# A decoder layer on one core: a ring of ten weight parts, a seventh seven-product chunk, and one norm tile moved off VectorE

## The chip, the cores and the metric

The kernel runs on one core of a Trainium2 chip. The metric is the device time of one execution in microseconds (us). Engines are called PE (TensorE, the matrix engine), DVE (VectorE), ACT (ScalarE), POOL (GpSimd) and SP (SyncE, which here only issues DMAs). "L159" is line 159 of the kernel before.

## The reference

One layer for 256 tokens of width 1024, with 256 memory tokens and an inner width of 2816. Each of its three parts ends in a residual sum and a layer norm:

```python
z = h @ w_in                                  # pooling inputs u, and q, k, v of the attention
mix = concat(multiscale_pool(u), moba_attention(q, k, v)) @ w_out
h = layer_norm(ALPHA * h + mix, ln1_g, ln1_b)
h = layer_norm(ALPHA * h + memory_cross_attention(h, mem, w_xq, w_xkv, w_xo), ln2_g, ln2_b)
h = layer_norm(ALPHA * h + (silu(h @ w_gate) * (h @ w_up)) @ w_down, ln3_g, ln3_b)

def layer_norm(x, g, b):
    mu = mean(x, -1); var = mean((x - mu) ** 2, -1)
    return (x - mu) * rsqrt(var + 1e-5) * g + b
```

All arrays are float32.

## The kernel before, in words

**Products.** A float32 product is made of three PE products in a format that keeps fewer bits: each operand is cast to a high part (`h` in the names), the rest is its low part (`l`), and high x high, high x low and low x high are added in PSUM (`three`, L328 to L330). So every weight must be split before PE can use it: ACT casts the high part (L157) and DVE subtracts it from the original (L159).

**The stream of weights.** The class `Stream` (object `ws`) treats all weights as one list of numbered parts of 512 KB, 128 partitions x 1024. Part i is fetched by a DMA that SP issues into a raw tile `w{i}r` (a ring of seven), and split into `w{i}h` and `w{i}l` (a ring of `W_BUFS` = 8). `ws.prepare(n)` issues the splits up to part n, and the kernel calls it with `ws.used + AHEAD`, where `used` counts the parts with which PE is done, and `AHEAD` is 8. So the split of part i waits for PE's last product with part i-8. Small loads, as those of norm vectors, are hung in front of a part's fetch (`ws.before`).

**Gate and up.** Parts 59 to 102 hold the gate and up weights of the chunks c = 0 to 10 (256 of the 2816 inner columns each; four parts to a chunk). `proj_both` runs a chunk in phases: a group of rows first with the high parts (L775), then with the low parts (L781). A part counts as used in the low phase only. The group is all eight rows for most chunks and two rows for the last two. While PE works on a chunk, DVE and ACT finish the one before: `Gated.add` (L929, L930), `multiply` (L934, L935), and `split` (L391, L392), which gives the two parts of the activations of the chunk. Tokens go in two tiles of 128, t = 0 and 1.

**Down.** The down weights of a chunk are two parts, and a chunk costs 24 products of 128x512 (`eight`). For a chunk in the tuple `SEVEN`, the 2x2 block product (two token tiles by two halves of the columns) is instead done in seven block products of sums of blocks, so 21 PE products (`seven`). Its weights then need sums, which `prepare_pair` makes: three ring parts and a corner tile `w{i}c`, with eight DVE operations (L125 to L136) in place of two. `Gated.split` makes the sums of its activations (L946 to L949) and splits them too. Chunks are taken in the order `DOWN`. The last three, `LAST`, are plain and are kept for the end.

**The tail.** When the other chunks are done, DVE forms the residual plus the shared block products (L1061 to L1074). Meanwhile PE runs `pieces`: the six last parts for tile 0's lower and upper half, for tile 1's lower half, and for two quarters of tile 1's upper half. The first of these pieces is the first to use a last part, so it needs all six splits. As each piece ends, DVE adds it (L1090) and takes its statistics (L675). When a tile is complete, `finish` runs `stats` (L680, L682 on DVE, then the power -1/2 on POOL, L683, which gives `rs`), `centre` (L688: subtract the mean, multiply by g), `scale` (L693, in three pieces: multiply by `rs`, add b) and the stores (L986).

**Order.** The program is written out in order for each engine, and each engine takes its instructions strictly in that order; waits follow from the tiles' data and from the rings. Activations live in a ring of eleven tiles of 8 KB a partition (`a8`), smaller ones in rings of their own. The norm's vectors g and b and its two rows `r` have a pool of their own (`nmp`), in the space that the `early` pool gives back before the mix.

Of the kernel before, what the change touches and what calls it, by code (L numbers as in the profile page):

```python
# [24 lines left out]
NFC = DFF // CW  # L25
# [15 lines left out]


# [4 lines left out]
class Stream:  # L47
# [3 lines left out]
    def __init__(self, nc, pool):  # L51
        self.nc, self.pool = nc, pool
        self.pairs, self.corner = {}, {}
        self.src, self.raws, self.tiles, self.homes = [], [], [], []
        self.loads, self.splits = {}, {}
        self.used, self.held = 0, True
        self.pace, self.asked = 1, 0
        self.cuts, self.casts = {}, {}

    def add(self, src, parts=2):  # L60

# [23 lines left out]
    def fetch(self, upto, queue):  # L85

        while len(self.raws) < min(upto, len(self.src)):
            i = len(self.raws)
            for load in self.loads.pop(i, []):
                load()  # L90
            src = self.src[i]
            if src is None:
                self.raws.append(None)
                continue
            if i < len(self.homes):
                raw = self.homes[i]
            else:
                raw = self.pool.tile(list(src.shape), F32, tag="raw", name=f"w{i}r", bufs=RAW_BUFS)
            for s, q in self.cuts.get(i, [(slice(None), queue)]):
                q.dma_start(raw[:, :, s], src[:, :, s])  # L100
            self.raws.append(raw)

    def fetch_ahead(self):

# [33 lines left out]
    def prepare(self, upto, eng=None):  # L138
        nc = self.nc
        while len(self.tiles) < min(upto, len(self.src)):  # L140
            i = len(self.tiles)
            src = self.src[i]
            for split in self.splits.pop(i, []):
                split()
            self.fetch(i + 1, nc.sync)
            raw = self.raws[i]
            shape = list((self.src[i - 1] if src is None else src).shape)
            hi = self.pool.tile(shape, F32R, tag="hi", name=f"w{i}h")
            lo = self.pool.tile(shape, F32R, tag="lo", name=f"w{i}l")
            if i in self.pairs:  # L150
                self.prepare_pair(i, hi, lo)
                self.tiles.append((hi, lo))
                self.fetch_ahead()
                continue
            for group in self.casts.get(i, [[slice(None)]]):
                for s in group:
                    nc.scalar.copy(hi[:, :, s], raw[:, :, s])  # L157
                s = slice(group[0].start, group[-1].stop)
                (eng or nc.vector).tensor_sub(lo[:, :, s], raw[:, :, s], r32(hi[:, :, s]))  # L159
            self.tiles.append((hi, lo))  # L160
            self.fetch_ahead()

    def next(self):

        if not self.held:
            self.prepare(min(self.used + AHEAD, len(self.tiles) + 1))

    def get(self, numbers, k):

        n = self.src[numbers[0]].shape[1]  # L170
        self.prepare(numbers[k // n] + 1)
        self.asked += 1
        if not self.held and self.asked % self.pace == 0:
            self.prepare(min(self.used + AHEAD, len(self.tiles) + 1))
        return self.parts_of(numbers, k)

    def parts_of(self, numbers, k):
# [16 lines left out]
def decoder_layer(  # L194
# [24 lines left out]
    ws = Stream(nc, wp)  # L219
# [29 lines left out]
    c_gu = [ws.add(w_gu[c], 4) for c in range(NFC)]  # L249
    c_dn = {}  # L250
# [37 lines left out]
        nc.sync.dma_start(wpl, w_pool)  # L288
        nc.sync.dma_start(psc, pool_scale)

    gb = {}
# [360 lines left out]


    early.close()
    nmp = ctx.enter_context(tc.tile_pool(name="norm", bufs=1))


    class Norm:
        def __init__(self, i, tok, dst=None):
# [31 lines left out]
        def scale(self, c0, c1):  # L691
            s = slice(c0, c1)
            nc.vector.scalar_tensor_tensor(self.dst[:, s], self.r[:, s], self.rs, gb["b", self.i][:, s],  # L693
                                           op0=OP.mult, op1=OP.add)
# [11 lines left out]
    def project(chunks, get, held, pieces=PIECES):  # L706

        acc = {piece: accbank("acc") for piece in PIECES}  # L710
        if pieces != PIECES:
            (*_, (_, _, c), _), last = pieces, PIECES[-1]
            acc[pieces[-2]], acc[pieces[-1]] = acc[last][:, :c - last[1]], bank("acc")[:, :last[2] - c]
        head, rest = chunks[:-held], chunks[-held:]
        done = sum(ws.rows(numbers) for numbers in head)
        if head:
            yield from proj_rows(acc, head, get, PIECES, True, pieces != PIECES, True)
        ws.prepare(ws.used + AHEAD)
        ws.prepare(ws.used + W_BUFS, nc.gpsimd)
# [15 lines left out]
    h1 = ap.tile([P, T, D], F32, tag="a8", name="h1")  # L735
    mix = project(c_mix, lambda k: (cT[0][:, k], cT[1][:, k]), 4)
    for t in range(T):
        norm = Norm(1, xt[:, t, :], h1[:, t, :])
        for half in HALVES:
            norm.add(*half, until(mix)[1])  # L740
        norm.finish()
# [105 lines left out]
    h2T = Both("h2T")  # L847
# [11 lines left out]
    xattend(3)  # L859


    norm = Norm(2, h1[:, 0, :], h2[:, 0, :])
    for half in HALVES:
        norm.add(*half, until(xo)[1])
    norm.finish()
    norm = Norm(2, h1[:, 1, :], h2[:, 1, :])
# [17 lines left out]
    def gated_parts(c):  # L884


        if c in SEVEN:
            t = ap.tile([P, 2, 8, P], F32R, tag="a8", name=f"g{c}")
            gT[c] = t[:, 0], t[:, 1]
            return  # L890
        i, j = divmod([c for c in sorted(DOWN) if c not in SEVEN].index(c), 2)
        if j == 0:
            shared[i] = ap.tile([P, 2, 8, P], F32R, tag="a8", name=f"go{i}")
        gT[c] = tuple(shared[i][:, n, 4 * j:4 * j + 4] for n in range(2))

    def gated_pair(c, k, t):

# [87 lines left out]
    def store(t, y, c0, c1, queue=nc.sync):  # L985
        queue.dma_start(out[t * P:(t + 1) * P, c0:c1], y[:, c0:c1])  # L986
# [68 lines left out]


    lower, upper = slice(0, 512), slice(512, D)
    norms = [Norm(3, h2[:, t, :]) for t in range(T)]

    def with_residual(t, s, y):  # L1060
        nc.vector.scalar_tensor_tensor(norms[t].r[:, s], h2[:, t, s], ALPHA, y, op0=OP.mult, op1=OP.add)  # L1061
# [16 lines left out]
    def finish(norm, t):  # L1078

        norm.stats()  # L1080
        norm.centre(0, D)
        norm.scale(0, 512)
        store(t, norm.r, 0, 512)
        norm.scale(512, 768)
        store(t, norm.r, 512, 768, nc.scalar)
        norm.scale(768, D)
        store(t, norm.r, 768, D)

    def add(norm, c0, c1, acc):
        nc.vector.tensor_add(norm.r[:, c0:c1], acc, norm.r[:, c0:c1])  # L1090
# [69 lines left out]
```

## Time and profile before

| | |
|---|---|
| time, median of 3 runs | 379.52 us (379.52 to 379.84) |
| profiled execution | 380.66 us, its span 378.9 us, so 1.76 us lie around the span |
| granted PE clock, mean | 0.992 |
| PE busy | 368.3 us, 97% of the span, 2154 instructions |
| DVE busy | 303.1 us, 80%, 475 instructions |
| ACT busy | 200.3 us, 53%, 316 instructions |
| POOL busy | 20.4 us, 5%, 31 instructions |
| DMA | 71.95 MB, mean 190 GB/s |

A row of the timeline gives the start of an instruction within the span, its length, engine, line, operation, output and inputs, and in brackets how long its engine had been idle before it and what it waited for. Lengths of neighbours overlap a little, so the cost of one among many is the distance of two starts. In the rows of groups, the numbers behind the bar are the busy time of all and the mean length of one in ns.

### The profile page before, as it was taken

What the parts mean: (1) busy time and instruction counts of PE and PEld (TensorE: products, weight loads), DVE (VectorE), ACT (ScalarE), POOL (GpSimd) and SP (SyncE); (2) the same over time, 40 slices, a digit from 0 to 9 for tenths busy, and PEclk for the clock granted to TensorE, in tenths of its full rate; (3) what the DMA queues carried; (4) which work ended last, traced back from release to release, by engine and by line L of the source; (5) the groups of instructions that cost most, each with busy time, mean ns of one, the idle gap of its engine ahead of it and who ended that gap; (6) DMA issues with size and microseconds to landing.
All of it is one profiled execution on the core that took longest, in us unless ns stands there. A gap on an engine that the chain in (4) does not pass through costs nothing.

```text
span 378.9 us, 5741 instructions
## 1 busy us (share of the span) xinstructions
PE 368.3 (97%) x2154; PEld 323.3 (85%) x2154; DVE 303.1 (80%) x475; ACT 200.3 (53%) x316; POOL 20.4 (5%) x31
## 2 busy tenths in 40 slices
PE   8999999999999999999999999999999999999990
PEld 7997989998888889998878888888888888888880
DVE  4867889955599677865889787778886998999995
ACT  4746678643254645644147666555665565456400
POOL 1000035300020000000100000000000000000011
PEclk9999999999999999999999999999999999999996
DMA  8997683759508963343107855566554663364002
GB/s 263 412 411 252 205 293 129 228 179 299 191 3 270 390 215 123 113 161 112 61 3 240 331 171 173 196 222 220 193 167 163 260 221 111 111 222 136 32 35 78
DMA packets 21324, 71.95 MB, mean 190 GB/s; under 512 B 2480, under 2 KB 3504, under 8 KB 21168
## 3 DMA queue, kind: packets, MB, share of 16 engines
q1 hardware_dynamic: 20720, 71.05, 54.5%
q10 hardware_dynamic: 576, 0.52, 0.4%
q8 instruction: 17, 0.28, 0.3%
q14 instruction: 11, 0.09, 0.1%
HBM read 70.52 MB, written 1.05 MB: 189 GB/s over the span
## 4 chain that ended last, share of the span: by engine, by line
PE 90%; DVE 5%; ACT 1%; DMA 1%; POOLq 0%; POOL 0%; SPq 0%; issue 0%; DVEq 0%; ACTq 0%
PE pg L775 19%; PE pg L781 10%; PE pxk L346 6%; PE pqk L462 5%; PE pxq L775 4%; PE acc L328 4%; PE acc L329 4%; PE acc L330 4%; PE pu L346 3%; PE m L330 3%; PE m L329 3%; PE m L328 3%; PE pxq L781 2%; PE xv L330 2%; PE xv L329 2%; PE xv L328 2%
## 5 line engine op out<-in xcount | busy, mean ns | idle before, releaser
L683 POOL TENSOR_TENSOR rs<-rs,mhalf 128x1 f32<-128x1 f32 x6 | 6.4, 1070 | 297.2 <-DVE rs L682 297.2
L391 ACT CAST g<-sg 128x512 fp32r<-128x512 f32 x12 | 7.4, 621 | 15.1 <-DVE sg L949 10.1
L392 DVE TENSOR_TENSOR g<-sg,g 128x512 fp32r<-128x512 f32 x12 | 8.3, 693 | 8.2 <-ACT g L391 8.2
L929 ACT COPY sg<-pg 128x256 f32<-128x256 f32 x40 | 12.0, 385 | 4.6 <-PE pg L781 4.4
L930 DVE TENSOR_TENSOR sg<-pg,sg 128x256 f32<-128x256 f32 x40 | 14.1, 413 | 0.0
L934 ACT ACTIVATE sg<-sg 128x512 f32<-128x512 f32 x10 | 6.4, 636 | 13.7 <-DVE sg L930 13.7
L498 ACT ACTIVATE xpr<-xs,mx 128x256 f32<-128x256 f32 x8 | 3.7, 470 | 14.3 <-DVE mx L509 14.3
L498 ACT ACTIVATE pr<-pr,mx 128x128 f32<-128x128 f32 (+1 forms) x16 | 7.1, 444 | 6.8 <-DVE mx L529 6.8
L675 DVE BATCH_NORM_STATS2 st<-r 128x6 f32<-128x512 f32 (+1 forms) x16 | 9.0, 561 | 0.5
L391 ACT CAST h2T<-tp 128x512 fp32r<-128x512 f32 x4 | 2.3, 587 | 13.1 <-PE tp L419 13.1
L688 DVE SCALAR_TENSOR_TENSOR r<-r,mv,g 128x512 f32<-128x512 f32 (+1 forms) x10 | 8.2, 849 | 0.0
L935 DVE TENSOR_TENSOR sg<-sg 128x512 f32<-128x512 f32 x10 | 6.9, 692 | 0.9
L503 DVE RECIPROCAL sm<-sm 128x2 f32<-128x2 f32 x12 | 2.0, 166 | 6.0 <-ACT xpr L498 4.5
L573 POOL TENSOR_TENSOR win<-win 128x269 f32<-128x269 f32 (+2 forms) x6 | 6.5, 1082 | 0.5
L573 POOL TENSOR_TENSOR win<-upad 128x271 f32<-128x271 f32 x4 | 3.5, 872 | 54.9 <-ACT upad L601 54.9
L807 PE MATMUL xs<-xkTh,xq 128*128 128x256 f32 x32 | 6.4, 282 | 0.0
L693 DVE SCALAR_TENSOR_TENSOR h<-r,rs,b 128x512 f32<-128x512 f32 x8 | 5.7, 744 | 0.5 <-DVE r L688 0.5
L391 ACT CAST h1T<-tp 128x512 fp32r<-128x512 f32 x4 | 2.4, 588 | 7.1 <-PE tp L419 7.1
L807 PEld LDWEIGHTS xs<-xkTh,xq 128*128 128x128 f32 x32 | 5.2, 191 | 0.2
L157 ACT CAST w39h<-w39r 128x1024 fp32r<-128x1024 f32 x1 | 1.1, 1060 | 7.8 <-PE acc L330 7.8
L419 PEld LDWEIGHTS tp<-ident,h 128*128 128x128 f32 x32 | 3.9, 141 | 1.3 <-issue 0.4
L391 ACT CAST xkTh<-pxk 128x512 fp32r<-128x512 f32 x4 | 2.4, 588 | 4.9 <-PE pxk L346 4.9
(1167 smaller groups left out, 1370.4 us busy)
## 6 DMA issues: line engine op xcount, KB each, us to landing
g<-in_ln_g SPq DMA_DIRECT2D x3, 512.0 KB, 5.4
b<-in_ln_b SPq DMA_DIRECT2D x3, 512.0 KB, 7.1
wr<-in_w_qkv SPq DMA_DIRECT2D x5, 256.0 KB, 5.8
mr<-in_mem_t SPq DMA_DIRECT2D x1, 1024.0 KB, 11.3
xt<-in_x SPq DMA_DIRECT2D x1, 1024.0 KB, 8.3
xr<-in_x_t SPq DMA_DIRECT2D x3, 256.0 KB, 7.2
wr<-in_w_qkv SPq DMA_DIRECT2D x1, 512.0 KB, 7.2
w7r<-in_w_qkv SPq DMA_DIRECT2D x1, 512.0 KB, 7.7
```

The lines of the kernel that those rows point to most:

```text
L328: nc.tensor.matmul(ps, wa, ya, start=start, stop=False, skip_group_check=part)
L329: nc.tensor.matmul(ps, wa, yb, start=False, stop=False, skip_group_check=part)
L330: nc.tensor.matmul(ps, wb, ya, start=False, stop=stop, skip_group_check=part)
L346: nc.tensor.matmul(pss[f], w[:, s], y, start=k == 0 and f == 0 and n == 0, stop=k == KD - 1 and n == 2, skip_group_check=True)
L391: nc.scalar.copy(h, ps)
L462: nc.tensor.matmul(qk[i][:, f, :], w[:, c * P:(c + 1) * P], y, start=k == 0 and f == 0 and w is hi and y is x_hi, stop=k == KD - 1 and w i ...
L498: nc.scalar.activation(dst[:, j, :], src[:, j, :], AF.Exp, bias=mx[:, j:j + 1], scale=sign, accum_out=sm[:, j:j + 1])
L775: nc.tensor.matmul(ps, hi[:, b * P:(b + 1) * P], yT.both(k), start=k == 0, stop=False, skip_group_check=True)
L781: nc.tensor.matmul(ps[:, S:], lo[:, b * P:(b + 1) * P], yT.pair(k)[0], start=False, stop=k == KD - 1, skip_group_check=True)
L807: nc.tensor.matmul(ps[:, t, :], q[:, kk, t * P:(t + 1) * P], k[:, 2 * h + kk], start=n == 0, stop=q is q_lo and kk == 1, skip_group_check= ...
L929: nc.scalar.copy(y[:, f, :], ps[:, S:])
L930: nc.vector.tensor_add(y[:, f, :], ps[:, :S], y[:, f, :])
```

## The change

Four things are changed together.

- *The ring.* From the mix on, two more slots for split parts exist, in a pool `late` that takes the space of `early`. `AHEAD` becomes `ws.ahead`, ten from then on.
- *Norm tiles.* The vectors g and b of a norm become one tile of the `a8` ring, and the two rows `r` another. The third norm's vectors are loaded in front of the parts of the first of the `LAST` chunks, instead of in front of the third and fourth down chunk.
- *Down.* Chunk 7 joins `SEVEN`, so chunk 0 is the only plain one ahead of the `LAST` three, and the order is 1, 2, 0, 3 to 7, then 8, 9, 10. Gate and up of chunk 8 also go in groups of two rows. The activations of chunks 9 and 10 get tiles of their own.
- *The last norm.* For tile 0, `apart` replaces centre and scale: DVE only makes `less`, the negated mean; ACT adds it (in two halves of 512 columns), POOL multiplies by g, ACT multiplies by `rs`, POOL adds b; so POOL has two products and two sums of 128x512 in its queue, between the two tiles' powers. Tile 0's two stores go out on SP. Tile 1 is done as before.

Core of the diff:

```diff
-RAW_BUFS, W_BUFS, AHEAD = 7, 8, 8
+RAW_BUFS, W_BUFS, LATE_BUFS = 7, 8, 2
...
-DOWN = (1, 0, 2, 3, 4, 7, 5, 6, 8, 9, 10)
-SEVEN = (1, 2, 3, 4, 5, 6)
+DOWN = (1, 2, 0, 3, 4, 5, 6, 7, 8, 9, 10)
+SEVEN = (1, 2, 3, 4, 5, 6, 7)
...
+    def widen(self, pool):
+        self.late, self.ahead = (len(self.tiles), pool), W_BUFS + LATE_BUFS
...
-            hi = self.pool.tile(shape, F32R, tag="hi", name=f"w{i}h")
-            lo = self.pool.tile(shape, F32R, tag="lo", name=f"w{i}l")
+            pool = self.pool
+            if self.late and (i - self.late[0]) % self.ahead < LATE_BUFS:
+                pool = self.late[1]
+            hi = pool.tile(shape, F32R, tag="hi", name=f"w{i}h")
+            lo = pool.tile(shape, F32R, tag="lo", name=f"w{i}l")
...
-            self.prepare(min(self.used + AHEAD, len(self.tiles) + 1))
+            self.prepare(min(self.used + self.ahead, len(self.tiles) + 1))
...
-            gb[tag, i] = nmp.tile([P, D], F32, tag=tag, name=f"{tag}{i}")
+            if i not in gbs:
+                gbs[i] = ap.tile([P, 2, D], F32, tag="a8", name=f"gb{i}")
+            gb[tag, i] = gbs[i][:, "gb".index(tag), :]
...
-    ws.before(c_dn[DOWN[2]][0], load_norm("g", 3, ln3_g))
-    ws.before(c_dn[DOWN[3]][0], load_norm("b", 3, ln3_b))
+    ws.before(c_dn[LAST[0]][0], load_norm("g", 3, ln3_g))
+    ws.before(c_dn[LAST[0]][1], load_norm("b", 3, ln3_b))
...
-    nmp = ctx.enter_context(tc.tile_pool(name="norm", bufs=1))
+    ws.widen(ctx.enter_context(tc.tile_pool(name="late", bufs=LATE_BUFS)))
...
-            self.r = nmp.tile([P, D], F32, name="r", bufs=2)
+            if t == 0:
+                rows_of[i] = ap.tile([P, T, D], F32, tag="a8", name=f"r{i}")
+            self.r = rows_of[i][:, t, :]
...
+        def apart(self):
+            less = sp.tile([P, 1], F32, name="less")
+            nc.vector.tensor_scalar(less, self.mv[:, 0:1], -1.0, None, op0=OP.mult)
+            g, b = gb["g", self.i], gb["b", self.i]
+            halves = [slice(*half) for half in HALVES]
+            for s in halves:
+                nc.scalar.activation(self.r[:, s], self.r[:, s], AF.Identity, bias=less, scale=1.0)
+                nc.gpsimd.tensor_mul(self.r[:, s], self.r[:, s], g[:, s])
+            for s in halves:
+                nc.scalar.activation(self.r[:, s], self.r[:, s], AF.Copy, bias=0.0, scale=self.rs)
+                nc.gpsimd.tensor_add(self.r[:, s], self.r[:, s], b[:, s])
+                yield s
...
-        gu = proj_both(pss, c_gu[c], h2T, KD if c < NFC - 2 else 2)
+        gu = proj_both(pss, c_gu[c], h2T, KD if c < NFC - 3 else 2)
...
         norm.stats()
+        if t == 0:
+            for s in norm.apart():
+                store(t, norm.r, s.start, s.stop)
+            return
         norm.centre(0, D)
```

More of the change, by code (lines that the diff above doesn't have):

```diff
@@ L58, in __init__ @@
         self.cuts, self.casts = {}, {}
+        self.late, self.ahead = None, W_BUFS
     def add(self, src, parts=2):
@@ L173, in get @@
         if not self.held and self.asked % self.pace == 0:
-            self.prepare(min(self.used + AHEAD, len(self.tiles) + 1))
+            self.prepare(min(self.used + self.ahead, len(self.tiles) + 1))
         return self.parts_of(numbers, k)
@@ L654, in decoder_layer, with __init__ @@
     early.close()
-    nmp = ctx.enter_context(tc.tile_pool(name="norm", bufs=1))
+    ws.widen(ctx.enter_context(tc.tile_pool(name="late", bufs=LATE_BUFS)))
+    rows_of = {}
     class Norm:
-        def __init__(self, i, tok, dst=None):
+        def __init__(self, i, t, tok, dst=None):
             self.i, self.tok = i, tok
-            self.r = nmp.tile([P, D], F32, name="r", bufs=2)
+            if t == 0:
+                rows_of[i] = ap.tile([P, T, D], F32, tag="a8", name=f"r{i}")
+            self.r = rows_of[i][:, t, :]
             self.dst = self.r if dst is None else dst
@@ L717, in project @@
             yield from proj_rows(acc, head, get, PIECES, True, pieces != PIECES, True)
-        ws.prepare(ws.used + AHEAD)
-        ws.prepare(ws.used + W_BUFS, nc.gpsimd)
+        ws.prepare(ws.used + ws.ahead)
+        ws.prepare(ws.used + ws.ahead, nc.gpsimd)
         ws.held = True
@@ L737, in decoder_layer @@
     for t in range(T):
-        norm = Norm(1, xt[:, t, :], h1[:, t, :])
+        norm = Norm(1, t, xt[:, t, :], h1[:, t, :])
         for half in HALVES:
@@ L859, in decoder_layer @@
     xattend(3)
-    norm = Norm(2, h1[:, 0, :], h2[:, 0, :])
+    norm = Norm(2, 0, h1[:, 0, :], h2[:, 0, :])
     for half in HALVES:
@@ L865, in decoder_layer @@
     norm.finish()
-    norm = Norm(2, h1[:, 1, :], h2[:, 1, :])
+    norm = Norm(2, 1, h1[:, 1, :], h2[:, 1, :])
     acc0 = until(xo)[1]
@@ L891, in gated_parts @@
         i, j = divmod([c for c in sorted(DOWN) if c not in SEVEN].index(c), 2)
-        if j == 0:
+        if i == 0 and j == 0:
             shared[i] = ap.tile([P, 2, 8, P], F32R, tag="a8", name=f"go{i}")
-        gT[c] = tuple(shared[i][:, n, 4 * j:4 * j + 4] for n in range(2))
+        if i == 0:
+            gT[c] = tuple(shared[i][:, n, 4 * j:4 * j + 4] for n in range(2))
+        elif j == 0:
+            gT[c] = tuple(sp.tile([P, 4, P], F32R, name=f"go{n}", tag="pr", bufs=PR_BUFS) for n in range(2))
+        else:
+            t = ap.tile([P, 2, 4, P], F32R, tag="a8", name=f"go{i}")
+            gT[c] = t[:, 0], t[:, 1]
     def gated_pair(c, k, t):
@@ L1057, in decoder_layer @@
     lower, upper = slice(0, 512), slice(512, D)
-    norms = [Norm(3, h2[:, t, :]) for t in range(T)]
+    norms = [Norm(3, t, h2[:, t, :]) for t in range(T)]
     def with_residual(t, s, y):
@@ L1080, in finish @@
         norm.stats()
+        if t == 0:
+            for s in norm.apart():
+                store(t, norm.r, s.start, s.stop)
+            return
         norm.centre(0, D)
[L1082 to L1087, printed above, removed]
+        for c0, c1, queue in ((0, 512, nc.sync), (512, 768, nc.scalar), (768, D, nc.sync)):
+            norm.scale(c0, c1)
+            store(t, norm.r, c0, c1, queue)
     def add(norm, c0, c1, acc):
```

2 lines of the change are left out of this document (1 added, 1 removed).

## The prediction

> **What bounds the kernel now.** I read the page's busy line first, then what TensorE (PE) waits for, then the windows of the last third, then the chain of waits, and last the timelines of VectorE (DVE), PE and GpSimd (POOL).
>
> ```profile
> PE 368.3 (97%) x2154; PEld 323.3 (85%) x2154; DVE 303.1 (80%) x475; ACT 200.3 (53%) x316; POOL 20.4 (5%) x31
> ```
>
> ```profile
> PE pqk L462 <- ACT w2h L157: 1.0, 1, 1.0
> PE busy L432 <- PEq L1124: 0.8, 1, 0.8
> ```
>
> The first row says that PE works 97% of the span; the two under it are all that PE waits for, both at the start. So up to the tail the time is PE's work, and nothing that only moves DVE, ACT or DMA work earlier can gain there. The average of 80% hides that DVE is full at the end, which the windows show (PE, PEld, DVE, ACT and POOL busy in each):
>
> ```profile
> core 0: us, PE busy (x) PEld busy (x) DVE busy (x) ACT busy (x) POOL busy (x), PEclk, DMA share, GB/s
> 202.50:291.80 89.30, 89.30 (x518) 79.12 (x517) 70.02 (x110) 54.87 (x86) 0.00 (x0) 1.00 0.61 208
> ...
> 330.00:349.00 19.00, 19.00 (x86) 15.73 (x85) 18.51 (x22) 10.57 (x12) 0.00 (x0) 1.00 0.53 170
> ```
>
> DVE has 19.3 us free in the gate and up chunks (89.30 - 70.02), but 0.5 in the 19 us of the down chunks. The chain that ended last leaves PE there:
>
> ```profile
> 348.68 0.24 PE m L330
> ...
> 355.47 1.14 DVE w130l L159
> ```
>
> From about 349 us on the chain is casts, then DVE, and no longer PE: the end is set jointly by DVE's queue and by PE's last pieces. A change that saves PE products gains only if DVE delivers the last weight part earlier too.
>
> **Part 1: the seventh chunk in seven products.** Chunk 7 goes from 24 products of 512 columns to 21.
>
> ```profile
> 356.68 0.39 PE L330 MATMUL m<-w129h,go 128*128 128x512 f32 x1
> ...
> 357.13 0.39 PE L329 MATMUL m<-w130l,go 128*128 128x512 f32 x1
> 357.36 0.39 PE L330 MATMUL m<-w130h,go 128*128 128x512 f32 x1
> ...
> 369.94 0.28 PE L330 MATMUL acc<-w130h,go 128*128 128x256 f32 x1
> ```
>
> Three products take 357.36 - 356.68 = 0.68 us, so PE is 0.68 earlier at each later point, if it is fed. The price is paid on DVE, in two places: the chunk's weights, and its activations.
>
> ```profile
> 274.89 0.28 DVE L946 TENSOR_TENSOR sg<-sg 128x128 f32<-128x128 f32 x1
> ...
> 276.59 0.69 DVE L392 TENSOR_TENSOR g<-sg,g 128x512 fp32r<-128x512 f32 x1 [0.69 <-ACT g L391]
> 277.96 1.22 DVE L159 TENSOR_TENSOR w95l<-w95r,w95h 128x1024 fp32r<-128x1024 f32 x1 [0.67 <-PE pg L781]
> ...
> 289.07 1.23 DVE L159 TENSOR_TENSOR w99l<-w99r,w99h 128x1024 fp32r<-128x1024 f32 x1 [2.98 <-PE pg L781]
> ...
> 333.31 1.22 DVE L159 TENSOR_TENSOR w117l<-w117r,w117h 128x1024 fp32r<-128x1024 f32 x1
> 334.45 1.22 DVE L159 TENSOR_TENSOR w118l<-w118r,w118h 128x1024 fp32r<-128x1024 f32 x1
> 335.58 0.68 DVE L125 TENSOR_TENSOR w119c<-w119r,w119c 128x512 fp32r<-128x512 f32 x1
> ...
> 342.65 0.69 DVE L125 TENSOR_TENSOR w122c<-w122r,w122c 128x512 fp32r<-128x512 f32 x1
> ...
> 355.39 1.21 DVE L159 TENSOR_TENSOR w130l<-w130r,w130h 128x1024 fp32r<-128x1024 f32 x1
> ```
>
> A chunk in seven takes DVE 342.65 - 335.58 = 7.07 us; a plain part takes 334.45 - 333.31 = 1.14. Splitting the sums of a chunk's activations, which a plain chunk doesn't need, runs from 274.89 to 276.59 + 0.61 (the step between two such operations, estimated as half a plain part's with its overlap) = 277.20, so 2.3 us, 0.69 of it a wait for ACT.
>
> **Part 2: the ring of ten, and chunk 8 in groups of two.** Part i may now be split once PE has finished part i-10, not i-8. Up to gate and up this gains nothing, since PE waits for nothing there, and costs nothing: the same releases drive the same number of splits, two parts further on. What it can do is fill DVE's idle time. Of that the rows show one large piece, the 2.98 us before w99l: DVE waits for the low phase of chunk 8, which frees its slots only after the whole high phase.
>
> ```profile
> 280.74 7.28 PE pg L775 x32
> 288.02 3.83 PE pg L781 x32
> ```
>
> In groups of two, the first slot comes free after a quarter of the 7.28 and of the 3.83, at about 283.5, and the ring asks for it two parts later. So the 2.98 go entirely. PE executes the same 64 matmuls, at no cost.
>
> Now DVE's queue from 277.96 on, where the ring wait (on chunk 7's low phase) is the same event in both kernels. Before, the parts from w95 to w130 follow: 18 plain ones and 6 triples. After, w97 to w131 follow: 14 plain ones and 7 triples. The difference is 7.07 - 4 x 1.14 = +2.5; with the splitting +2.3 and the idle time -2.98 that is +1.8, less some 0.1 for rounding in the overlaps: I take +1.7. DVE is otherwise full between these two points, so nothing else is there to be filled. The last part, w130l before at 355.39, becomes w131l at 355.39 + 1.7 = 357.1, done at 358.3. PE wants its low half where w130l stood at 357.13, less 0.68: at 356.45. **It stalls about 1.9 us.** From that product to the start of the last one is 369.94 - 357.13 = 12.81, so PE ends at 358.35 + 12.81 + 0.28 = 371.44. This is the step on which the forecast stands; its error is that of a small difference of large sums, and I bound it by one wait for ACT of the kind shown (0.69) each way.
>
> **Part 3: the first norm tile off VectorE.** The tail of DVE before:
>
> ```profile
> 356.52 0.68 DVE L1061 SCALAR_TENSOR_TENSOR r<-h,m 128x512 f32<-128x512 f32 x1
> ...
> 365.12 0.15 DVE L682 TENSOR_SCALAR rs<-mv 128x1 f32<-128x1 f32 x1
> 365.19 1.28 DVE L688 SCALAR_TENSOR_TENSOR r<-r,mv,g 128x1024 f32<-128x1024 f32 x1
> 366.91 1.54 DVE L693 SCALAR_TENSOR_TENSOR r<-r,rs,b 128x512 f32<-128x512 f32 x3 [0.44 <-POOL rs L683]
> 368.37 0.42 DVE L1090 TENSOR_TENSOR r<-m,r 128x256 f32<-128x256 f32 x1
> ...
> 371.06 0.41 DVE L1090 TENSOR_TENSOR r<-acc,r 128x256 f32<-128x256 f32 x1
> ...
> 374.05 1.54 DVE L693 SCALAR_TENSOR_TENSOR r<-r,rs,b 128x512 f32<-128x512 f32 x3 [0.44 <-POOL rs L683]
> ```
>
> PE's last product ended at 369.94 + 0.28 = 370.22, and the last add began at 371.06: DVE was 0.84 late, because tile 0's centre, wait and scale held it for 368.37 - 365.19 = 3.18 us. After the change these 3.18 leave DVE. Its tail begins 1.72 later (358.24 for 356.52), reaches tile 0's `rs` at 366.84, adds `less` (0.07 of queue) and is at tile 1's adds at about 366.9, where it used to be at 368.37. From there PE is the later one, and the last add waits for PE until 371.45. That is **+0.39** on 371.06. So the saving of 3.18 becomes 1.5 of lead, then waiting for PE.
>
> What takes the work over, and whether it is in time:
>
> ```profile
> 54.81 0.63 POOL L573 TENSOR_TENSOR win<-upad 128x271 f32<-128x271 f32 x1
> ...
> 56.24 0.22 POOL L575 TENSOR_TENSOR win<-win,fac 128x16 f32<-128x16 f32 x1
> ...
> 192.51 0.55 POOL L683 TENSOR_TENSOR rs<-rs,mhalf 128x1 f32<-128x1 f32 x1 [5.50 <-DVE rs L682]
> ...
> 372.56 1.45 POOL L683 TENSOR_TENSOR rs<-rs,mhalf 128x1 f32<-128x1 f32 x1 [5.68 <-DVE rs L682]
> ```
>
> ```profile
> L573 POOL TENSOR_TENSOR win<-win 128x257 f32<-128x257 f32 x1 | 1.6, 1606 | 0.1
> L934 ACT ACTIVATE sg<-sg 128x512 f32<-128x512 f32 x10 | 6.4, 636 | 13.7 <-DVE sg L930 13.7
> ```
>
> POOL first runs tile 0's power, at about 367.14. No centre runs on DVE beside it now, so I take 0.55 (the row at 192.51), not 1.45: done at 367.7. ACT subtracts the mean of the first half in 0.64 from about 367.2 (the L934 row; a plain function of this size is not shown dearer), so the first product starts at 367.9. Four products of 512 columns follow on POOL; ACT's scaling of one half lies under POOL's product for the other. A product of 512 is not in the trace. The line through 0.22 at 16 and 0.63 at 271 columns gives 0.22 + 496 x 0.41 / 255 = 1.02; in proportion to 271 it is 1.19; the dearest row, 1.606 for 257 columns, is the upper bound. I take 1.1, because DVE's adds in that stretch read one operand from PSUM: POOL is free at 372.3. Tile 1's power stands behind these four on POOL, and DVE's three scales and the last stores wait for it; nothing else is queued there. It is asked for at 372.56 + 0.39 = 372.95, so it finds POOL free and the tail after it keeps its length.
>
> The row and the rule for this place: the power took 0.55 beside other work and 1.45 beside tile 1's centre at its start. The Trainium skill, SBUF — State Buffer, section Who interferes with whom, says why that may be: a VectorE instruction with two SBUF inputs and a GpSimd instruction that reads SBUF take turns, and the second blocks. By that rule a product that is still running at 372.7 would also hold back tile 1's centre; by the rows alone only the power is late.
>
> **Part 4: what I cost at nothing.** The norm vectors and rows move to the activation ring; their slots' former users ended long before. The load of the third pair of vectors moves from two early down chunks to the parts of chunk 8:
>
> ```profile
> 334.56 0.33 SPq L100 DMA_DIRECT2D w126r<-in_w_down  x1
> ```
>
> ```profile
> b<-in_ln_b SPq DMA_DIRECT2D x3, 512.0 KB, 7.1
> ```
>
> It is issued near 335 and lands 7.1 us later, 25 us ahead of its first use at 367.9; the parts behind it on SP are asked for at DVE's pace, and the cover would be gone only if w131r came later than 357. Tile 0's two stores on SP go out at about 371.2 and 372.3, ahead of tile 1's first at 374.8: free as long as POOL ends by then.
>
> **The sum.** PE -0.68, stall for DVE's last part +1.9, DVE's lateness in the tail -0.84: +0.4. The profiled execution took 380.66 (span 378.9), so it would take 381.05; it stands 1.14 over the median of 379.52, to which I add the same: **379.9 us**. About 0.2% (0.76 us) is what a measurement of this kernel can tell from no change. With the ends of the disputed step (0.69 each way) this case reaches from 379.2 to 380.6.
>
> **Rivals.** *GpSimd becomes the tail.* The four products cost more than taken, tile 1's power starts late, and with it scale and stores. It decides from (372.95 - 367.9) / 4 = 1.26 us per product on, and surely from 1.5 (tile 1's centre ends near 374.0 and blocks the power until then in any case, so it must start by 373.9). At 1.61, POOL is free at 374.3, and the scale starts at 374.9 (power 0.55) to 375.8 (1.45) for 374.05: +0.9 to +1.8, so 380.4 to 381.3, about 380.9. For it: POOL's rows beside DVE's weight splits are that dear; last product and tile 1's centre are within 0.4 us of each other. Against: between 367.9 and 372.3 DVE has no operation with two operands in SBUF.
>
> *VectorE keeps up.* If the ring's two parts more of lead survive into the down chunks (more of DVE's idle time before 277.96 can be filled than I allow), w131l is there by 356.45, PE ends at 356.45 + 12.81 + 0.28 = 369.54 and the last add follows at once: 369.58 for 371.06, -1.5, so 378.0. For it: DVE has 19.3 us free in gate and up. Against: the wait at 277.96 is for PE, and the high phase of chunk 7 still goes unbroken.
>
> *Nothing happens.* The parts cancel, and the time stays at 379.5.
>
> **Chances.** The forecast 0.58 (0.40 within 0.2%, 0.15 slower, 0.03 faster); GpSimd 0.22 (0.20 slower, 0.02 within); VectorE keeps up 0.17 (faster); nothing 0.03 (within). Faster 0.20, same 0.45, slower 0.35. The range of 8 in 10 takes in the forecast's own, GpSimd's up to its end of 381.3, and of the faster case what lies over 378.5; left out are some 0.13 below and 0.05 above.
>
> **What would show it.** In the profile after: no idle time of DVE at chunk 8; w131l near 357.1; PE waiting 1 to 2 us for `w131l` in the first piece, which it never did before; the last add near 371.4 with a wait for PE; POOL products near 1.1 us and tile 1's power right behind DVE's `rs`. I am wrong if PE shows no wait in the pieces (the faster rival), or if the power waits for POOL's own queue or the products are over 1.26 (the slower one).

## The result, and the profile after

The changed kernel takes 380.95 us (median of 6 runs, 380.61 to 381.42), the kernel before 379.68 beside it (379.48 to 380.41): ratio 1.0032, 95% interval 1.0019 to 1.0045. So it is slower by 1.27 us, in the forecast range (378.5 to 381.3) and on the side of the forecast, but by three times the forecast's 0.4.

The profile of before that the prediction was read from has PE wait 1.0 us for its first weights. A second profile of the same kernel (e1 below) hasn't, so it is the one to hold beside the profile after: in both, the first product with the V weights (`pv`) starts within 0.04 us, as the timelines of PE show, e1 first. In the other runs it starts up to 0.8 us later. So where two runs are compared "from V on" below, the start of this product is taken off each time.

```profile
27.43 0.40 PE L328 MATMUL pv<-w11h,xTh 128*128 128x512 f32 x1
```

```profile
27.47 0.40 PE L338 MATMUL pv<-w11h,xTh 128*128 128x512 f32 x1
```

The line of busy shares of the page after, and those waits of PE that are new (us in total, times, longest):

```profile
PE 369.4 (98%) x2151; PEld 322.4 (85%) x2151; DVE 306.9 (81%) x483; ACT 204.6 (54%) x323; POOL 24.5 (6%) x35
```

```profile
PE m L339 <- DVE w131l L167: 0.2, 1, 0.2
PE m L339 <- DVE w129l L167: 0.2, 1, 0.2
PE m L339 <- DVE w130l L167: 0.2, 1, 0.2
```

PE has three instructions fewer, and is busy 1.1 us longer. (In e1 it is busy 368.1 us.) Its waits for the last low halves are there, but this view gives them only 0.2 us each; what they cost is seen in the timeline of PE:

```profile
354.08 0.50 PE L339 MATMUL m<-w128l,go 128*128 128x512 f32 x1
...
355.21 0.50 PE L339 MATMUL m<-w129l,go 128*128 128x512 f32 x1 [0.17 <-DVE w129l L167]
...
356.34 0.50 PE L339 MATMUL m<-w130l,go 128*128 128x512 f32 x1 [0.17 <-DVE w130l L167]
...
357.48 0.50 PE L339 MATMUL m<-w131l,go 128*128 128x512 f32 x1 [0.17 <-DVE w131l L167]
...
370.42 0.28 PE L340 MATMUL acc<-w131h,go 128*128 128x256 f32 x1
```

From part to part it is 1.13 us, the pace of DVE's splits, where three products take 0.68. From the first product with a last part to the last product of all it is 18.05 us (352.37 to 370.42), in e1 16.43 (352.26 to 368.69): the stall costs 1.62 us. The chain that ended last shows the same: casts, the last two splits, then PE up to the last add.

```profile
355.07 1.22 DVE w130l L167
356.29 1.15 DVE w131l L167
357.48 0.50 PE m L339
...
370.58 0.13 PE acc L340
370.74 0.44 DVE r L1125
```

The tail on DVE after, and the same places in the second profile of before:

```profile
356.21 1.22 DVE L167 TENSOR_TENSOR w131l<-w131r,w131h 128x1024 fp32r<-128x1024 f32 x1
...
365.95 0.15 DVE L696 TENSOR_SCALAR rs<-mv 128x1 f32<-128x1 f32 x1
...
366.43 0.42 DVE L1125 TENSOR_TENSOR r<-m,r 128x256 f32<-128x256 f32 x1 [0.26 <-PE m L340]
...
370.74 0.42 DVE L1125 TENSOR_TENSOR r<-acc,r 128x256 f32<-128x256 f32 x1 [0.94 <-PE acc L340]
...
373.74 1.54 DVE L707 SCALAR_TENSOR_TENSOR r<-r,rs,gb 128x512 f32<-128x512 f32 x3 [0.44 <-POOL rs L697]
```

```profile
354.14 1.22 DVE L159 TENSOR_TENSOR w130l<-w130r,w130h 128x1024 fp32r<-128x1024 f32 x1
...
369.83 0.41 DVE L1090 TENSOR_TENSOR r<-acc,r 128x256 f32<-128x256 f32 x1
```

The last split starts 2.07 us later, the last add 0.91 later (from V on 2.03 and 0.88), and it now waits for PE. POOL in the tail after:

```profile
366.25 0.55 POOL L697 TENSOR_TENSOR rs<-rs,mhalf 128x1 f32<-128x1 f32 x1 [174.05 <-DVE less L713]
367.00 2.56 POOL L718 TENSOR_TENSOR r<-r,gb 128x512 f32<-128x512 f32 x2 [0.20 <-ACT r L717]
369.51 2.51 POOL L721 TENSOR_TENSOR r<-r,gb 128x512 f32<-128x512 f32 x2
372.25 1.45 POOL L697 TENSOR_TENSOR rs<-rs,mhalf 128x1 f32<-128x1 f32 x1 [0.23 <-DVE rs L696]
```

Its four operations come 1.26 us apart, and it is idle for 0.23 us before tile 1's power: in time, with little to spare.

### The profile page after: what moved, and what is told of

The parts are those of the page before. It is cut to its first block, busy times and chain, and to the rows that moved or that the text cites. A ratio compares the mean times of both kernels' runs of the same rounds, so it can differ in the third digit from the quotient of the medians.

```text
span 378.5 us, 5753 instructions
## 1 busy us (share of the span) xinstructions
PE 369.4 (98%) x2151; PEld 322.4 (85%) x2151; DVE 306.9 (81%) x483; ACT 204.6 (54%) x323; POOL 24.5 (6%) x35
## 4 chain that ended last, share of the span: by engine, by line
PE 95%; ACT 1%; DVE 1%; POOLq 0%; issue 0%; DVEq 0%; ACTq 0%
PE pg L803 19%; PE pg L809 10%; PE pqk L472 6%; PE pxk L356 6%; PE m L339 4%; PE acc L338 4%; PE acc L339 4%; PE acc L340 4%; PE m L340 4%; PE m L338 4%; PE pxq L803 4%; PE pu L356 3%; PE pxq L809 2%; PE xv L338 2%; PE xv L340 2%; PE xv L339 2%
## 5 line engine op out<-in xcount | busy, mean ns | idle before, releaser
L697 POOL TENSOR_TENSOR rs<-rs,mhalf 128x1 f32<-128x1 f32 x6 | 5.5, 920 | 293.8 <-DVE less L713 174.0
L401 ACT CAST g<-sg 128x512 fp32r<-128x512 f32 x14 | 8.7, 620 | 17.4 <-DVE sg L983 12.4
L402 DVE TENSOR_TENSOR g<-sg,g 128x512 fp32r<-128x512 f32 x14 | 9.7, 692 | 8.9 <-ACT g L401 8.9
L717 ACT ACTIVATE r<-r,less 128x512 f32<-128x512 f32 x2 | 1.3, 714 | 10.7 <-DVE less L713 10.7
L702 DVE SCALAR_TENSOR_TENSOR r<-r,mv,gb 128x512 f32<-128x512 f32 (+1 forms) x9 | 7.0, 803 | 0.0
L707 DVE SCALAR_TENSOR_TENSOR h<-r,rs,gb 128x512 f32<-128x512 f32 x8 | 5.7, 748 | 0.1
L165 ACT CAST w41h<-w41r 128x1024 fp32r<-128x1024 f32 x1 | 1.1, 1057 | 7.9 <-PE acc L340 7.9
L402 DVE TENSOR_TENSOR h1T<-tp,h1T 128x512 fp32r<-128x512 f32 x4 | 2.8, 689 | 2.8 <-ACT h1T L401 2.8
```

The source lines that it names most:

```text
L401: nc.scalar.copy(h, ps)
L402: nc.vector.tensor_sub(l, ps, r32(h))
```

## The experiments

In the short diffs, the lines are those of the kernel that the experiment starts from.

**e1, the kernel before once more**, for its profile; no edit.

> The kernel before, unchanged, for a second profile. In its first profile PE waited 1.0 us for w2h near the start, and its profiled execution (380.66 us) stood 1.14 us over its median; in the profile after this wait is not there. Theory A (that wait is a late first transfer, which most executions do not have): the second profile shows no such wait, its span is near 377.8 us, and the last add of the tail (first 371.06) begins near 370.0. Theory B (the wait belongs to the kernel): it is there again and the span is 378.9 us. Time 379.5 to 379.9 us in both.

379.93 us, ratio 0.9996 (0.9988 to 1.0005); span 377.6, no wait for w2h, last add at 369.83. Theory A. Outside the span lie 379.44 - 377.6 = 1.84 us of its profiled execution; of the changed kernel's, 380.67 - 378.5 = 2.17. Over all runs it is 1.74 to 1.90 and 2.11 to 2.18 us. So 0.33 us of the slowdown are not in the span at all.

**e2, the added ring slots moved by 32 bytes.**

```diff
-            less = sp.tile([P, 1], F32, name="less")
+            less = sp.tile([P, 1], F32, name="less", bufs=2)
```

> The changed kernel with the two added ring slots moved down by 64 bytes less 32, that is, to addresses of the same remainder by 64 as the other eight slots (210784 in place of 210816); nothing else. In the profile after, products of 512 columns whose weights lie in the added slots (parts 104, 105, 114, 115, 124, 125) come 0.2333 us apart, all others 0.2267. Theory A (the place within 64 bytes makes them slow): all are 0.2267 apart again, and the time falls by what PE lost on the way, about 0.7 us, from 380.95 to 380.2. Theory B (the region of memory, or the deeper ring itself): still 0.2333, time 380.95 within 0.2.

380.77 us, ratio 1.0024 (1.0016 to 1.0033), theory B: parts 114 and 115 still come at 0.233 us a product. The place within 64 bytes is not the cause of that pace. The shift is not without effect, though: from V on, PE starts with part 116 (`w116h`) 0.64 us later than e1 in the changed kernel, 0.46 later here, and 1.04 later in e6, where the tile `less` is missing and the slots lie lower too. The reading behind the pace, in the timeline of PE of the changed kernel:

```profile
333.82 0.40 PE L338 MATMUL m<-w114h,g 128*128 128x512 f32 x1
...
336.62 0.39 PE L338 MATMUL m<-w116h,g 128*128 128x512 f32 x1
...
338.00 0.39 PE L338 MATMUL m<-w117c,g 128*128 128x512 f32 x1
...
340.04 0.39 PE L338 MATMUL m<-w118h,g 128*128 128x512 f32 x1
```

Parts 114 and 115 lie in the added slots: 12 products in 2.80 us, 0.233 each. Part 117 doesn't: 9 in 2.04, 0.227. In gate and up, chunk 1 has parts 64 and 65 in added slots, as stationary operands; the chain of before (e1) and of after:

```profile
201.30 7.26 PE pg L775 x32
```

```profile
201.56 7.36 PE pg L803 x32
```

The low phase that follows is 0.06 us shorter after (3.85 for 3.91), so of the 0.10 little is left: most of the loss comes from parts that are the moving operand.

**e3, the ring of eight all the way.**

```diff
-    ws.widen(ctx.enter_context(tc.tile_pool(name="late", bufs=LATE_BUFS)))
```

> The changed kernel with the ring of eight all the way; chunk 8 stays in groups of two, the seventh chunk and the norm tile stay changed. By the prediction's part 2 the 2.98 us of idle time are filled by groups and ring together. Theory A (the groups alone free a slot by 283.5, which is when VectorE comes to it; the two added slots only slow PE): w131l is done where it is after (357.4 less nothing), no product is over 0.2267 apart, time about 0.7 us under the changed kernel, 380.2. Theory B (the ring is what lets VectorE run on): VectorE idles 1 to 3 us for the ring around chunk 8, w131l is late by that, and the time is 382 to 384 us.

384.17 us, ratio 1.0111 (1.0097 to 1.0125). Theory A falls. PE now waits in earlier chunks too:

```profile
PE m L339 <- DVE w124l L138: 0.9, 1, 0.9
PE m L339 <- DVE w123l L133: 0.7, 1, 0.7
PE m L339 <- DVE w121l L138: 0.6, 1, 0.6
```

```profile
359.36 1.22 DVE L167 TENSOR_TENSOR w131l<-w131r,w131h 128x1024 fp32r<-128x1024 f32 x1
```

The last split starts 3.15 us later than after, 2.65 from V on (V is at 27.96 here). Theory B has the time, but only part of the reason: the wait of 2.98 us is gone with the ring of eight too, so the groups of two alone remove it. DVE is two parts further back when it comes to be full (w95l starts at 277.09 here, w97l at 277.12 after), so 2 x 1.14 = 2.3 us late. From V on it starts there 0.5 earlier, and its waits from there to the last split sum to 3.6 us for 2.7 after: 2.3 - 0.5 + 0.9 = 2.7. What theory A said of the slots is borne out: without them PE starts with part 116 0.09 us ahead of e1, from V on, for 0.64 behind it in the changed kernel. Given the seventh chunk, the deeper ring is worth about 3 us, slow slots included (3.2 by the medians, 3.0 by the ratios, 2.6 by the two spans from V on).

**e4, only the norm tile moved**, in the kernel before: `apart` and its call added, nothing else.

> The kernel before with only the last norm's first tile moved to ScalarE and GpSimd; ring of eight, six chunks in seven. Theory A (VectorE was 0.84 us late behind PE's last product in the tail, by the work that leaves it): the last add follows PE's last product at once, time 379.68 - 0.84 = 378.8 us, ratio 0.998. Theory B (GpSimd's four operations at 1.26 us each come so late that tile 1's power waits for them): the gain is eaten up, time 379.5 to 380.3 us.

379.2 us, ratio 0.9984 (0.9975 to 0.9993). Timeline of DVE and POOL:

```profile
369.27 0.42 DVE L1105 TENSOR_TENSOR r<-acc,r 128x256 f32<-128x256 f32 x1 [0.94 <-PE acc L330]
```

```profile
370.79 1.45 POOL L683 TENSOR_TENSOR rs<-rs,mhalf 128x1 f32<-128x1 f32 x1 [0.52 <-DVE rs L682]
```

The last add waits for PE. Its first V product is 0.28 later than in e1, so it gained 369.83 - 369.27 + 0.28 = 0.84, as expected. Outside the span it has 379.2 - 377.0 = 2.2 us, which takes back 0.35. This part of the change alone makes the kernel faster.

**e5, the added slots at the low end of memory**, raw tiles at the high end.

```diff
+    rp = ctx.enter_context(tc.tile_pool(name="raws", bufs=RAW_BUFS, side="right"))
-    wp = ctx.enter_context(tc.tile_pool(name="weights", bufs=W_BUFS))
+    wp = ctx.enter_context(tc.tile_pool(name="weights", bufs=W_BUFS, side="right"))
...
```

(The pools of activations and small tiles go to the right as well, `early` and then `late` stay left.)

> The changed kernel with another layout of memory: the two added ring slots lie at the low end (928 to 17312 bytes of a partition), and the raw tiles, which PE never reads, at the high end (200672 to 229344); order of work and rings unchanged. Theory A (PE reads weights more slowly out of the highest 16 KB, whatever the ring): parts 104, 105, 114, 115, 124, 125 come 0.2267 us apart, and the time falls by 0.6 to 0.7 us from 380.9 to 380.3. Theory B (a deeper ring is itself what slows PE, by more work of the other engines beside it): still 0.2333, time 380.9.

380.7 us, ratio 1.0026 (1.0015 to 1.0036): neither theory as it stood. The added slots are as slow at 928 to 17312 as at 210816 to 227200. But corner tiles, which this layout moved from 185248 to 197536 down to 19456 to 31744, have become slow as well. (The places follow from the order and sizes of the pools in the kernels.) PE on the corner of part 111, in the changed kernel and in e5:

```profile
328.38 0.39 PE L338 MATMUL m<-w111c,g 128*128 128x512 f32 x1
...
329.06 0.39 PE L338 MATMUL m<-w111h,g 128*128 128x512 f32 x1
```

```profile
328.83 0.40 PE L340 MATMUL m<-w111c,g 128*128 128x512 f32 x1
...
329.54 0.39 PE L340 MATMUL m<-w111h,g 128*128 128x512 f32 x1
```

Three products take 0.68 us there and 0.71 here. Parts 114, 120 and 123 show the same; the corners of 106 and 117, which follow slow parts, leave it open. Since the order of work is the same and only the layout differs, the pace goes with the place in memory. A deeper ring by itself (theory B) doesn't explain it: the products with the other eight slots keep 0.227, apart from a few right behind a slow part, and in e3 all of these parts do. Slow places are found near both ends, fast ones at 29600 to 95136 (before and after) and in the main at 135136 to 200672 (here). Where the limits lie, whether the place of the other operand counts, and why it is so, isn't shown.

**e6, tile 0 back on DVE** (the call of `apart` taken out).

> The changed kernel with the last norm's first tile back on VectorE (ring of ten and seventh chunk stay). Theory A (the forecast's part 3: 3.18 us return to VectorE between tile 0's statistics and tile 1's adds, of which 1.5 us were lead over PE): the last add begins at 366.0 + 3.2 + 2.7 = 371.9 for 370.74, the time rises by 1.15 us to 382.1. Theory B (GpSimd's queue already cost the changed kernel about as much): the power is no longer behind GpSimd's sums, and the time stays at 380.9.

382.16 us, ratio 1.0068 (1.0056 to 1.0081), by the medians 1.2 us over the changed kernel, by the ratios 1.4. Theory A; but that its time is hit so closely is luck. Timeline of DVE (V is at 28.24):

```profile
357.35 1.22 DVE L167 TENSOR_TENSOR w131l<-w131r,w131h 128x1024 fp32r<-128x1024 f32 x1
...
373.03 0.41 DVE L1121 TENSOR_TENSOR r<-acc,r 128x256 f32<-128x256 f32 x1
```

From V on the last add is 1.52 us later than after. Of that, 0.37 is a later last split, since PE comes later to each part here (see e2), and the other 1.15 is what theory A named. Outside the span lie 1.82 us for 2.17, which gives the 0.35 back.

**e7, six chunks** in seven, with `DOWN` and `SEVEN` as before; ring, groups and norm tile as after.

> The changed kernel with six chunks in seven and the old order of down (ring of ten, groups of two for chunk 8 and the norm tile stay). Theory A (the forecast's part 1: the seventh chunk saves PE 0.68 us and makes it stall 1.9 for VectorE's last part): no wait of PE for a low half in the pieces, time 380.9 - 1.2 = 379.7 us; the slow added slots still cost their 0.7. Theory B (the seventh chunk is worth its 0.68 and the loss is elsewhere): time 381.6 us.

379.73 us, ratio 1.0001 (0.9992 to 1.0010). Theory A; PE waits for no low half. Timeline of DVE (V is at 27.62):

```profile
350.04 1.22 DVE L167 TENSOR_TENSOR w130l<-w130r,w130h 128x1024 fp32r<-128x1024 f32 x1
...
369.95 0.42 DVE L1125 TENSOR_TENSOR r<-acc,r 128x256 f32<-128x256 f32 x1 [0.92 <-PE acc L340]
```

Ring and groups bring DVE's last split forward by 354.14 - 350.04 = 4.1 us, 4.3 from V on; the seventh chunk then puts it back by 356.21 - 350.04 = 6.2, 6.3 from V on. The last add comes 0.94 us earlier than after, from V on; the rest of the 1.2 lies outside the span (1.81 us for 2.17). Beside e4, which has the old ring, PE comes to the last add 369.95 - 369.27 = 0.68 us later, 0.77 from V on, though it waits for nothing: the price of the slow slots and the regrouping.

**e8, chunks 6 and 7 in groups of two too**, on top of e5.

```diff
-        gu = proj_both(pss, c_gu[c], h2T, KD if c < NFC - 3 else 2)
+        gu = proj_both(pss, c_gu[c], h2T, KD if c < NFC - 5 else 2)
```

> As e5, with chunks 6 and 7 of gate and up in groups of two as well. If VectorE's late last part is what is left (theory A), freeing the ring's slots earlier lets it put weight splits into its waits for ScalarE (0.69 us each, two for each chunk): w131l comes 1 to 2 us earlier against the products, PE's stall of 1.9 us shrinks to about 0.5, and the time is 1.2 us under e5, about 379.1. If VectorE is full from chunk 6 on in any case (theory B), the time is that of e5, plus 0.1 for the regrouping.

380.65 us, ratio 1.0029 (1.0018 to 1.0040), the time of e5. Theory B in time. In the two profiles the last split and the last add come 0.37 us earlier than in e5, from V on: from chunk 6 on there is little left to fill.

**e9, the first two pieces together**, in the changed kernel.

```diff
+        for c in LAST:
+            for k, number in enumerate(c_dn[c]):
+                ...
+                for n in (2, 3):
+                    into(n, gated_pair(c, k, t), pair(ws.tiles[number], ALL, 0, slice(first, last)))
```

> The changed kernel with the first two pieces of the tail (tile 0's lower and upper half) taken together, part by part: six products to a part instead of three, so PE comes to w131l 3.6 us later while VectorE delivers a part each 1.14 us. Nothing else changes. Theory A (the stall of 1.9 us for VectorE's last parts is what the seventh chunk costs): PE waits for no low half, ends 1.9 us earlier, VectorE is then the later one in the tail, the last add begins near 369.4 for 370.74, tile 1's power meets GpSimd still in tile 0's last sum (it ends at 372.0), and the time falls by about 1.1 us to 379.7. Theory B (the stall is hidden by VectorE's tail in any case): time 380.8 within 0.2.

381.2 us, ratio 1.0037 (1.0022 to 1.0052). PE waits for no low half, and the last add starts 1.49 us earlier than after (1.58 from V on), as theory A has it. From the first product with a last part to the last product it is 16.46 us, as in e1. But the time doesn't fall. DVE, then POOL:

```profile
369.25 0.42 DVE L1134 TENSOR_TENSOR r<-acc,r 128x256 f32<-128x256 f32 x1 [0.24 <-PE acc L340]
...
370.54 1.45 DVE L702 SCALAR_TENSOR_TENSOR r<-r,mv,gb 128x1024 f32<-128x1024 f32 x1
373.65 1.55 DVE L707 SCALAR_TENSOR_TENSOR r<-r,rs,gb 128x512 f32<-128x512 f32 x3 [1.66 <-POOL rs L697]
```

```profile
369.65 3.46 POOL L721 TENSOR_TENSOR r<-r,gb 128x512 f32<-128x512 f32 x2
373.07 0.54 POOL L697 TENSOR_TENSOR rs<-rs,mhalf 128x1 f32<-128x1 f32 x1
```

Tile 1's centre and tile 0's last sum now meet: the two sums take 3.46 us for 2.51, the power comes at 373.07, and the scale starts at 373.65 for 373.74. All that PE gained is lost in POOL's queue. This is the prediction's GpSimd rival; it takes over once the stall is gone.

**e10, the norm tile shared out**, in e4: POOL keeps the power and the products by g, DVE scales.

```diff
     norm.measure(512, 768)
+    for half in HALVES:
+        norms[0].scale(*half)
+        store(0, norms[0].r, *half)
```

> As e4 (kernel before with the first norm tile off VectorE), but VectorE does that tile's two scales, in its wait for PE ahead of the last add; GpSimd keeps the power and the two products by g, and is free at 367.8 instead of 370.3. Kernels in which GpSimd's sums end within 0.6 us ahead of tile 1's power have 2.13 to 2.19 us outside the span, the others 1.81 to 1.84. Theory A (GpSimd's late work is what adds those 0.35 us): outside the span 1.81, the last add at 369.5 (0.25 later, since two scales of 0.61 do not quite fit in 0.94), time 379.1. Theory B (it is the few stores close together): outside the span 2.19 still, time 379.45.

379.29 us, ratio 0.9987 (0.9977 to 0.9997); outside the span 378.85 - 377.1 = 1.75 us in its profiled execution, 1.75 to 1.92 in all of its runs. Theory A on the time outside the span: it goes with POOL's late work (in e7, where POOL has all four operations but is done 1.81 us before tile 1's power, it is 1.81 us). What that work does there isn't in the trace. The time is that of e4: what is gained outside the span is lost on the last add.

**e11, e9 with chunks 6 and 7 in groups of two.**

> As e9, with chunks 6 and 7 of gate and up in groups of two as well, which brought w131l 0.6 us forward in e8. Theory A (with the stall gone VectorE's tail sets the end, so its earlier start counts): 0.3 to 0.6 us under e9, about 379.3, held back by GpSimd, which is free 0.6 us earlier too. Theory B (PE sets the end): time of e9 plus 0.1.

380.57 us, ratio 1.0018 (1.0010 to 1.0027), 0.6 us under e9 by the medians. Theory A only in part, and not its time of 379.3: the scale starts at 373.29 for 373.65. The centre of tile 1 shows why (1.28 us alone):

```profile
370.54 2.31 DVE L702 SCALAR_TENSOR_TENSOR r<-r,mv,gb 128x1024 f32<-128x1024 f32 x1
```

**e12, e10 with tile 1's centre in two halves.**

```diff
-        norm.centre(0, D)
+        for half in HALVES:
+            norm.centre(*half)
```

> As e10, with tile 1's centre in two halves of 512 columns instead of one of 1024. In every kernel so far tile 1's power takes 1.45 us beside that centre (0.55 alone), and the scale waits 0.44 us for it. Theory A (VectorE and GpSimd take turns by whole instructions, so the power gets in after the first half): the power ends near 371.8 for 372.3, the scale of the first half starts 0.3 to 0.4 us earlier, time 0.3 under e10, about 378.9. Theory B (the power waits for both halves, or the second half waits for it as long): the scale starts where it did or 0.1 to 0.5 later, time 379.3 to 379.8.

378.62 us, ratio 0.9968 (0.9957 to 0.9980): theory A, and the fastest of all, 1.2 us under the kernel before. DVE and POOL:

```profile
370.52 1.41 DVE L688 SCALAR_TENSOR_TENSOR r<-r,mv,g 128x512 f32<-128x512 f32 x2
371.84 1.54 DVE L693 SCALAR_TENSOR_TENSOR r<-r,rs,b 128x512 f32<-128x512 f32 x3
```

```profile
370.75 0.92 POOL L683 TENSOR_TENSOR rs<-rs,mhalf 128x1 f32<-128x1 f32 x1 [3.28 <-DVE rs L682]
```

The power gets in behind the first half and is done in 0.92 us, so the scale no longer waits for it. From V on the scale starts 0.41 us earlier than in e10; the medians differ by 0.67. (In e9 and e11, tile 1's power had already taken other times than the 1.45 us of the expectation: 0.54 and 1.55.)

## Why the prediction was right, and where it was short

**The step it stood on held.** VectorE's last part was forecast 1.7 us later, with PE paced by it. It came 2.03 later, from V on, and PE goes through the last four parts at VectorE's pace of 1.13 us. The queue itself was counted well: from the first split that needs a slot of chunk 7 to the last split it takes 354.14 - 276.71 = 77.43 us in e1 and 356.21 - 277.12 = 79.09 after, so +1.66 for the forecast's 1.7. DVE in e1, then after:

```profile
276.71 1.23 DVE L159 TENSOR_TENSOR w95l<-w95r,w95h 128x1024 fp32r<-128x1024 f32 x1 [0.66 <-PE pg L781]
```

```profile
277.12 1.22 DVE L167 TENSOR_TENSOR w97l<-w97r,w97h 128x1024 fp32r<-128x1024 f32 x1 [0.27 <-ACT w97h L165]
```

Its terms fared less well one by one. Ring and groups alone brought the last split forward by 4.3 (e7), where the working has 2.98 + 2 x 1.14 = 5.3, and the seventh chunk put it back by 6.3 for 7.07 - 2 x 1.14 + 2.3 = 7.1. In e7 VectorE waits 1.60 us before w107l, as it does neither in e1 nor after; with the seventh chunk this wait is filled. That is the greater part of both errors, and in the sum they cancel. That the stall is what the seventh chunk costs is shown by e7 and e9; that undoing it gave back just the 1.2 us of the working (1.9 less 0.68) is partly luck, since 0.36 of it lies outside the span.

**Part 3 held.** Alone, the norm tile brings the last add forward by the 0.84 of the forecast (e4). After the change tile 1's adds wait for PE three times (0.26, 0.48 and 0.94 us), where before they never waited: so VectorE's lead became waiting, as forecast. POOL's operations took 1.26 us, not the 1.1 that I took between 1.02 and 1.19: the line through two rows of 16 and 271 columns was too low a bound, and so was the proportion. 1.26 is the very point from which the rival begins to count; POOL was in time by 0.23.

**Part 2 was mis-sized: the ring does not come free.** "Costs nothing" was argued from waits, of which there are none; what the added slots change is the pace of the products (e3, e5). In e1 the first product with a last part stands at 352.26; with 0.68 saved it should stand at 351.6, and it stands at 352.37.

```profile
352.26 0.39 PE L328 MATMUL m<-w125h,go 128*128 128x512 f32 x1
```

```profile
352.37 0.39 PE L338 MATMUL m<-w126h,go 128*128 128x512 f32 x1
```

So 0.75 us are lost on the way, from V on, and the term of -0.68 for PE came out as +0.07. What this does to the time goes through VectorE: its splits wait for PE up to chunk 7, so a slower PE makes VectorE late too. PE's last product with the low half of part 87 ends at 276.61 in e1 and at 277.03 after, and the two splits shown above follow 0.1 us behind it: 0.37 us later from V on (277.12 for 276.71, less the 0.04 of V). As PE came later to the last parts, the stall was 1.62 us and not 1.9.

**The time around the span was taken as constant**, and grew by 0.33 us.

Together: 0.39 of the forecast, 0.37 through the later split, and 0.13 because PE takes 12.94 us from the first product with w131l to the start of the last one (357.48 to 370.42), not the 12.81 of the working, make 0.89, where the last add shows 0.88 from V on. With the 0.33 outside the span that is 1.2 of the 1.27 us measured.

**The GpSimd rival** did not decide the changed kernel, but it stood right behind: removing the stall (e9) handed the end to it. The rule that I weighed there is that of the Trainium skill, SBUF — State Buffer, Who interferes with whom: VectorE with two SBUF inputs and a GpSimd instruction that reads SBUF take turns. The traces of e9, e11 and e12 agree with it: the centre took 1.45 and 2.31 us beside tile 0's last sums for 1.28, and a centre in two halves let the power in between.

## What to carry to other kernels

A saving on the engine that bounds the kernel counts only if the engine that feeds it can deliver its last piece earlier; count that feeder's queue, instruction by instruction, up to that piece. Work moved to an idle engine near the end must be done well before the last instruction that shares its queue, or its lateness comes back when the next wait is removed. Take a bundle of edits apart: here the norm tile alone gained 0.6 us (e4), the ring with the groups took that back (e7), and the seventh chunk on top of both lost 1.2. And before two traces are compared to a tenth of a microsecond, line them up on an instruction that the edit can't have moved.

## What the runs showed of the hardware

- PE's pace depends on where in a partition the weights lie. In down, where the weights are the moving operand, products of 512 columns come 0.233 us apart with weights from 210816 to 227200 bytes (after) and from 928 to 17312 (e5), and 0.227 from 29600 to 95136 (e1, after). Corner tiles are fast at 185248 to 197536 (after), and some of them slow at 19456 to 31744 (e5). With weights as the stationary operand, chunk 1's high phase takes 7.36 us for 7.26. Two such slots of ten cost PE 0.73 us up to part 116 (after against e3, from V on). A shift by 32 bytes (e2) leaves the pace in down, but PE's delay at part 116 is then 0.46 for 0.64 us.
- The power of one column on POOL takes 0.55 us alone, 0.92 between two halves of a centre and 1.45 beside a whole one that starts ahead of it.
- Kernels in which POOL works until shortly before tile 1's power have some 0.33 us more outside the span (2.17 for 1.84; 1.81 in e7, where POOL is done 1.81 us before that power).
